# A 32-byte pool at the right end of SBUF, under the tiles that the MLP and the scan keep there

## The chip, the cores and the metric

One core of one Trainium2 chip runs the whole program in one launch. The metric is the device time of that launch in microseconds (us), the median of several runs; lower is better. The engines named below are TensorE (PE; its weight loads are listed apart as PEld), VectorE (DVE), ScalarE (ACT), GpSimd (POOL) and SyncE (SP), whose queue issues the transfers (DMA). SBUF is the on-chip memory of 128 partitions; an address below is a byte within a partition, the same for all partitions.

## The reference

One layer of a hybrid backbone for 128 context tokens and 2,048 latent tokens, model width 1,024. All numbers are float32.

```python
h = rmsnorm(x, norm_mix) * (1 + sc1) + sh1
o, s_new = mixer(h, ...)        # one input projection; 4 heads of a bidirectional gated
                                # DeltaNet beside 4 groups of a chunked gMLP; one output projection
x = x + ga1 * o
h = rmsnorm(x, norm_ffn) * (1 + sc2) + sh2
x = x + ga2 * (square(relu(h @ w_ff1)) @ w_ff2)     # w_ff1 1024 x 4096, w_ff2 4096 x 1024
y = rmsnorm(x, norm_final)
```

The six vectors sh1 to ga2 come from a conditioning vector through `silu(c) @ w_mod + b_mod`. The outputs are y for both sequences and the final scan states of the context.

## The kernel before, in words

**Matmuls.** A float32 operand is split into a high and a low part of a shorter float type (`fp32r`), and a product is three matmuls, high by high, high by low, low by high. The helper `mm3` issues them, so that its three lines, L217, L218 and L219, carry nearly all matmuls of the profile. Of a matmul's two operands the moving one is streamed through TensorE, column by column, and the other, 128 by 128, is loaded first as weights. In a profile row `f<-hop,zH` the tile `hop` moves and `zH` is the weight.

**Stages.** The tokens form 17 tiles of 128 (`NT`). The first stage, to about 440 us, normalizes and projects; its moving operands are kH and kL, 388 columns, from a pool with 24 slots. The scan stage, to about 1300 us, runs the DeltaNet chunks in both directions and fills gaps with the gMLP and the output projection; an order written out by hand (`WINDOWS`) sets which step comes when. Then comes the MLP in two halves.

**First half of the MLP** (`Unit`, from about 1300 to 2032 us): each of 32 units covers 256 columns of w_ff1 for one half of the latent tokens. A Strassen-like scheme makes seven products of a unit, in the order 1, 5, 6, 7, 3, 2, 4 (`ORDER`); each is four k-tiles of three matmuls of 512 columns, with the token side `hop` moving and the weight side split on the fly (`split4`, L1452: ScalarE L1456 makes the high part, VectorE L1450 the low part). The units run in 28 blocks of one or two. There are seven `hop` tiles for each half of the tokens, fetched by `hop_next`; products 1 and 5 use the right side, the others the left.

**Second half** (from 2032 us to the end): seven products in turn (numbers 1, 5, 6, 7, 3, 4, 2), each visited for 8 or 9 pairs of token tiles. A visit is four quarters of four k-tiles, twelve matmuls a quarter. Now w_ff2 moves, from `hop` tiles that `t_build` fills, four k-tiles in each (a chunk): ScalarE copies the high part (L1632), VectorE makes the low part. The token side (`zraw` to `zH`, `zL`) is loaded again for every quarter, `AHEAD` and two more quarters early. A product has four chunks, so chunks 0 to 27 in all.

**Pools.** SBUF tiles come from stacked pools. Those on the left grow up from the constants (`const`, `small`, `wp`, ...), those on the right grow down from the end. On the right lies the pool `prep` in the scan stage (half-precision tiles AH, As, X, Y, P and some float32 ones) and, once it is closed (`swap_right`), the pool `hopA` with two `hop` tiles of 16,384 bytes. `hopB`, with five, lies on the left:

```python
side, bufs = ("A", 2) if n else ("B", 5)
return hops[side].tile([P, 4, 2, 512], dt, tag="hop", name="hop", bufs=bufs)
...
moved.append(hop_tile(F32R, (len(tcount) - 1) % 5 < 2))
```

Slots are rounded up to multiples of 32 bytes. The usable part of a partition ends at byte 229,344, which is 3583 times 64 and 32 more. So before the change `hopA` takes bytes 196,576 to 229,344 and all 26 slots of `prep` start at 32 above a multiple of 64. The five `hopB` tiles (from byte 113,024), the slots of `wp` (from 12,672) and those of the scan's left pools start on multiples of 64.

The two constants that the change touches: `nhalf`, a row of -0.5 that GpSimd uses as the exponent in `rsqrt_cols` (L172), at most 72 columns of it; `zcol`, eight zeros, read in the first stage for `abW` (L302) and for edge columns of kH and kL (L453).

Of the kernel before, what the change touches and what calls it, by code (L numbers as in the profile page):

```python
# [8 lines left out]
F32 = mybir.dt.float32  # L9
# [8 lines left out]
P = 128  # L18
D = 1024
KT = D // P  # L20
# [41 lines left out]
def hybrid_step(  # L62
# [21 lines left out]
        return ap.bitcast(F32)  # L84

    cp = ctx.enter_context(tc.tile_pool(name="const", bufs=1))
    dp = ctx.enter_context(tc.tile_pool(name="dram", bufs=1, space=DRAM))


# [23 lines left out]
    make_identity(nc, ident)  # L113
    ident16 = cp.tile([P, P], F16, name="ident16")
    V.tensor_copy(ident16, ident)
    nhalf = cp.tile([P, 72], F32, name="nhalf")
    V.memset(nhalf, -0.5)
    zcol = cp.tile([P, KT], F32, name="zcol")
    V.memset(zcol, 0.0)
    bd2 = cp.tile([P, P], F16, name="bd2")  # L120
    om = {w: cp.tile([P, P], F16, name=f"om{w}") for w in (2, 4, 8, 16, 32)}
# [138 lines left out]
    with ExitStack() as ph:  # L260
# [478 lines left out]
        side = []  # L739
        for bi in range(len(BLOCKS)):  # L740
# [8 lines left out]
            for n, (gi, h) in enumerate(order):  # L749
# [40 lines left out]
                side = []  # L790
# [114 lines left out]
    with ExitStack() as ph:  # L905
        right = ctx.enter_context(ExitStack())
# [1031 lines left out]
```

## Time and profile before

| what | value |
|---|---|
| time, median of 3 runs | 2715.29 us (2714.51 to 2718.88) |
| the profiled execution, first to last instruction | 2715.6 us |
| TensorE busy | 2631.7 us, 97% |
| TensorE weight loads | 2195.9 us, 81% |
| VectorE busy | 1867.8 us, 69% |
| ScalarE busy | 1247.8 us, 46% |
| GpSimd busy | 226.4 us, 8% |
| moved by transfers | 580.91 MB, mean 214 GB/s |
| mean granted TensorE clock | 0.990 |

The page lists busy time by engine, then the span in slices, the transfer queues, the chain of work that ended last, and the costliest groups of instructions. A group's row gives line, engine, operation, out<-in, shape and count, then busy time and the mean of one in ns, then the idle time of the engine just ahead of them and what ended it. Matmuls are pipelined: one's duration covers its way through the array, and the next starts before it ends, so the pace is read from the distance between starts, in the timeline. Other answers of the trace used below are the waits (who waited for whom, us in total, times, longest) and the table of stretches (busy time of each engine in a stretch of the span).

### The profile page before, as it was taken

Reading aid. Unit: us, or ns where it says so; the run is one execution under the profiler, and the core shown is the slowest. Engines: PE = TensorE matmul, PEld = TensorE weight load, DVE = VectorE, ACT = ScalarE, POOL = GpSimd, SP = SyncE. Lnnn points to the kernel's source line nnn. Section 1 sums busy time; section 2 is a strip of 40 time slices with the busy share of each in tenths; the row PEclk is TensorE's granted clock in tenths of the full one; section 3 lists DMA queues with packets and bytes.
Section 4 is the critical chain, followed back from the end, with each engine's and each line's share of the span. In section 5 each row is a group of like instructions: output and inputs, shape, how many; then the busy total and the mean of one; then the engine's idle time right before and its main releaser. Section 6 shows DMA issues by size and latency. Waiting matters only on the chain.

```text
span 2715.6 us, 45142 instructions
## 1 busy us (share of the span) xinstructions
PE 2631.7 (97%) x15682; PEld 2195.9 (81%) x15682; DVE 1867.8 (69%) x3911; ACT 1247.8 (46%) x3092; POOL 226.4 (8%) x448
## 2 busy tenths in 40 slices
PE   8999999999999999899999999999999999999998
PEld 4999998787887777778888778888888787788887
DVE  5867655877777879885677857665565556775874
ACT  4655555555555567763355533332342432332441
POOL 3112113111111111110000000000000000000000
PEclk9999999999999989999999999999999999999999
DMA  8867539555555657885877796333459978776782
GB/s 293 281 198 223 184 119 293 170 159 152 165 160 167 196 174 244 276 271 179 286 222 231 212 311 206 111 110 106 122 166 364 336 257 300 272 240 215 231 262 90
DMA packets 569387, 580.91 MB, mean 214 GB/s; under 512 B 35692, under 2 KB 401692, under 8 KB 565574
## 3 DMA queue, kind: packets, MB, share of 16 engines
q1 hardware_dynamic: 569158, 578.03, 66.9%
q8 instruction: 123, 2.02, 0.3%
q14 instruction: 106, 0.87, 0.1%
HBM read 398.14 MB, written 179.74 MB: 213 GB/s over the span
## 4 chain that ended last, share of the span: by engine, by line
PE 82%; DMA 7%; DVE 6%; issue 2%; ACT 1%; SPq 1%; POOL 0%; DVEq 0%; POOLq 0%; ACTq 0%
PE f L219 16%; PE f L217 16%; PE f L218 16%; PE pj L217 6%; PE pj L219 6%; PE pj L218 6%; PE pd L952 2%; DMA qT<-qT_d 2%; PE pm L217 1%; PE pm L219 1%; PE pm L218 1%; PE pd L1131 1%; DMA raw<-in_w_mod_dram 1%; PE pd L1132 1%; PE pt L568 1%
## 5 line engine op out<-in xcount | busy, mean ns | idle before, releaser
L219 PE MATMUL f<-hop,zL 128*128 128x512 f32 x960 | 377.6, 394 | 1.7 <-DVE zL L1450 1.7
L217 PE MATMUL f<-hop,zH 128*128 128x512 f32 x960 | 377.4, 393 | 1.7 <-ACT zH L1456 1.7
L218 PE MATMUL f<-hop,zH 128*128 128x512 f32 x960 | 377.5, 394 | 0.0
L217 PE MATMUL f<-hop,wH 128*128 128x512 f32 x896 | 356.2, 398 | 6.1 <-ACT wH L1456 6.1
L218 PE MATMUL f<-hop,wH 128*128 128x512 f32 x896 | 352.2, 393 | 0.0
L219 PE MATMUL f<-hop,wL 128*128 128x512 f32 x896 | 352.1, 394 | 0.0
L1456 ACT CAST zH<-zraw 128x512 fp32r<-128x512 f32 x240 | 147.0, 620 | 291.3 <-DVE zraw L1450 90.8
L217 PEld LDWEIGHTS f<-hop,zH 128*128 128x128 f32 x960 | 180.6, 188 | 45.4 <-ACT zH L1456 3.4
L219 PEld LDWEIGHTS f<-hop,zL 128*128 128x128 f32 x960 | 180.7, 188 | 45.0 <-DVE zL L1450 3.5
L218 PEld LDWEIGHTS f<-hop,zH 128*128 128x128 f32 x960 | 180.7, 188 | 41.1
L1450 DVE TENSOR_TENSOR zL<-zraw,zH 128x512 fp32r<-128x512 f32 x240 | 162.6, 686 | 67.9 <-ACT zH L1456 52.6
L217 PEld LDWEIGHTS f<-hop,wH 128*128 128x128 f32 x896 | 169.6, 189 | 41.3 <-ACT wH L1456 6.5
L219 PEld LDWEIGHTS f<-hop,wL 128*128 128x128 f32 x896 | 169.2, 189 | 38.1 <-DVE wL L1450 0.3
L218 PEld LDWEIGHTS f<-hop,wH 128*128 128x128 f32 x896 | 169.4, 189 | 35.4
L217 PE MATMUL pj<-kH,wH 128*128 128x386 f32 (+2 forms) x568 | 190.6, 338 | 0.6 <-DVE kH L466 0.3
L219 PE MATMUL pj<-kH,wL 128*128 128x386 f32 (+2 forms) x568 | 190.3, 335 | 0.0
L218 PE MATMUL pj<-kL,wH 128*128 128x386 f32 (+2 forms) x568 | 189.5, 334 | 0.0
L176 POOL TENSOR_TENSOR r<-rsq,nhalf 128x1 f32<-128x1 f32 (+1 forms) x38 | 23.1, 607 | 1520.8 <-DVE rsq L175 1520.8
L516 DVE SCALAR_TENSOR_TENSOR cv<-pj,vec,cv 128x384 f32<-128x384 f32 (+2 forms) x164 | 87.1, 539 | 60.4 <-ACT cv L513 56.5
L1450 DVE TENSOR_TENSOR wL<-raw,wH 128x512 fp32r<-128x512 f32 x112 | 76.1, 687 | 76.3 <-ACT wH L1456 75.3
L217 PEld LDWEIGHTS pj<-kH,wH 128*128 128x128 f32 x568 | 107.2, 189 | 5.2 <-issue 4.7
L218 PEld LDWEIGHTS pj<-kL,wH 128*128 128x128 f32 x568 | 107.5, 189 | 0.5
(404 smaller groups left out, 6083.0 us busy)
## 6 DMA issues: line engine op xcount, KB each, us to landing
zraw<-z_d SPq DMA_DIRECT2D x212, 256.0 KB
raw<-in_w_ff_dram SPq DMA_DIRECT2D x128, 256.0 KB
hop<-hop_d SPq DMA_DIRECT2D x28, 1024.0 KB
z_d<-c SPq DMA_DIRECT2D x96, 256.0 KB
zraw<-s_d SPq DMA_DIRECT2D x96, 256.0 KB
raw<-in_w_mod_dram SPq DMA_DIRECT2D x80, 256.0 KB
r<-in_w_ff_dram SPq DMA_DIRECT2D x80, 256.0 KB
s_d<-s SPq DMA_DIRECT2D x64, 256.0 KB
```

The source lines that it names most:

```text
L176: G.tensor_tensor(out=out, in0=t[:np_, :n], in1=nhalf[:np_, :n], op=ALU.pow)
L217: T.matmul(ps, lh, rh, start=first and i == 0, stop=False, skip_group_check=more)
L218: T.matmul(ps, lh, rl, start=False, stop=False, skip_group_check=more)
L219: T.matmul(ps, ll, rh, start=False, stop=last and i == n - 1, skip_group_check=more)
L516: V.scalar_tensor_tensor(out=cv[:, o : o + m], in0=ps[:, s + sh : s + sh + m], scalar=convw[:, w, j : j + 1], in1=cv[:, o : o + m], op0=AL ...
L568: T.matmul(ps[:, i * P : (i + 1) * P], kTt[:, i * P : (i + 1) * P], rhs[:, i * P : (i + 1) * P], start=True, stop=True)
L952: T.matmul(p[:, h, :], lhs[:, h, :], rhs[:, h, :], start=True, stop=True)
L1131: T.matmul(p[:, h, :], u["qT"][:, h, :], s[:, h, :], start=True, stop=False)
L1132: T.matmul(p[:, h, :], u["QK"][:, h, :], u["vn"][:, h, :], start=s is None, stop=True)
L1450: V.tensor_tensor(out=out, in0=a, in1=b, op=op)
L1456: A.copy(h, src)
```

## The change

A pool `edge` is opened on the right side ahead of all others, and `zcol`, 32 bytes a partition, moves there from the left. `nhalf` grows from 72 to 80 columns, by the 32 bytes that `zcol` leaves, so that all later tiles on the left keep their addresses. All on the right lies 32 bytes lower: the 26 slots of `prep` and the two `hop` tiles of `hopA` (now bytes 196,544 to 229,312) start on multiples of 64.

```diff
     cp = ctx.enter_context(tc.tile_pool(name="const", bufs=1))
+    edge = ctx.enter_context(tc.tile_pool(name="edge", bufs=1, side="right"))
...
-    nhalf = cp.tile([P, 72], F32, name="nhalf")
+    nhalf = cp.tile([P, 80], F32, name="nhalf")
     V.memset(nhalf, -0.5)
-    zcol = cp.tile([P, KT], F32, name="zcol")
+    zcol = edge.tile([P, KT], F32, name="zcol")
     V.memset(zcol, 0.0)
```

## Prediction

> **What bounds the kernel now.** I read the page first, then the groups of instructions by shape, then the table of stretches, then TensorE's timeline in one stretch of the MLP, and last the waits. The page gives the span and, in 40 slices, how busy the transfer engines are:
>
> ```profile
> span 2715.6 us, 45142 instructions
> ...
> DMA  8867539555555657885877796333459978776782
> ```
>
> The span, 2715.6 us, is 0.3 us above the median of the three runs, 2715.29 us (2714.51 to 2718.88), so the sum below is made against the profile and taken off the median as it stands. Transfers are near their limit in only some slices, the 30th and 31st above all.
>
> The groups say what the MLP is made of, 2,880 matmuls of 512 columns in its second half and 2,688 in its first, with the big `hop` tile as the moving operand in each:
>
> ```profile
> L217 PE MATMUL f<-hop,zH 128*128 128x512 f32 x960 | 377.4, 393 | 1.7 <-ACT zH L1456 1.7
> L218 PE MATMUL f<-hop,zH 128*128 128x512 f32 x960 | 377.5, 394 | 0.0
> L217 PE MATMUL f<-hop,wH 128*128 128x512 f32 x896 | 356.2, 398 | 6.1 <-ACT wH L1456 6.1
> ```
>
> Idle time ahead of them is 1.7 and 6.1 us in all. The duration of a matmul (393 ns) is no pace: the next starts long before it ends. The stretches (first the length, then busy time of PE, PEld, DVE, ACT, POOL, each with a count; granted clock, share of the transfer engines, GB/s) tell where TensorE sets the pace and where it does not:
>
> ```profile
> 1500.00:1620.00 120.00, 115.67 (x508) 94.48 (x507) 82.88 (x138) 53.18 (x110) 1.93 (x3) 0.97 0.80 250
> 1700.00:1800.00 100.00, 100.00 (x536) 85.67 (x535) 59.81 (x94) 31.21 (x58) 0.00 (x0) 1.00 0.39 111
> 2050.00:2070.00 20.00, 20.00 (x88) 16.28 (x87) 10.36 (x15) 5.47 (x9) 0.00 (x0) 1.00 1.02 369
> 2110.00:2130.00 20.00, 18.93 (x81) 15.07 (x82) 11.74 (x20) 12.23 (x23) 0.00 (x0) 1.00 1.00 354
> 2310.00:2320.00 10.00, 10.00 (x46) 8.15 (x45) 10.00 (x17) 6.43 (x11) 0.00 (x0) 1.00 1.06 392
> 2320.00:2330.00 10.00, 7.73 (x23) 4.69 (x22) 10.00 (x17) 3.10 (x5) 0.00 (x0) 0.83 1.01 358
> ```
>
> At 1700 TensorE is busy throughout and transfers take 0.39: whatever shortens a matmul there shortens the kernel. At 2050 to 2130 the transfers are full, and at 2110 TensorE waits 1.07 us. At 2320 VectorE and the transfers are full and TensorE waits 2.27 us.
>
> **What the moving tile costs.** In the second half a `hop` tile holds a chunk of four k-tiles: `t_build` puts chunk c into the right pair when c mod 5 is below 2, into the left five otherwise. Product 5 (the second) owns chunks 4 to 7, so in each of its visits quarters 1 and 2 read from the right pair, quarters 0 and 3 from the left five. These rows (start, duration) lie in its second visit:
>
> ```profile
> 2150.23 0.39 PE L217 MATMUL f<-hop,zH 128*128 128x512 f32 x1
> ...
> 2153.03 0.40 PE L217 MATMUL f<-hop,zH 128*128 128x512 f32 x1
> ...
> 2155.79 0.39 PE L217 MATMUL f<-hop,zH 128*128 128x512 f32 x1
> ...
> 2158.51 0.40 PE L217 MATMUL f<-hop,zH 128*128 128x512 f32 x1
> ```
>
> Each row starts the next twelve matmuls. Quarter 2, right pair: 2.80 us, 233.3 ns each. Quarter 3, left, directly behind it: 2.76 us. Quarter 0 of the next visit, left: 2.72 us, 226.7 ns each. So the right pair costs 6.7 ns a matmul, and another 0.04 us each time that work comes back to the left. The operands have the same shape, weights and neighbours. What differs is the address. Worked out from the declared sizes, the right end of the usable partition is byte 229,344, which is 32 above a multiple of 64, so both right tiles (16,384 bytes each) begin 32 above one; the five left tiles begin on multiples of 64.
>
> **Offset or place?** The right pair also lies at the far end, so this pair of stretches alone does not say that the offset is guilty. The first stage has a case inside one pool: the 24 slots of tag `h` are 1,568 bytes, 24.5 times 64, so that they alternate between offsets 0 and 32, and kH and kL sit on opposite ones. A triple reads kH twice and kL once. In the block at 181 us kH has offset 32, in the block at 262 us offset 0:
>
> ```profile
> 181.31 0.34 PE L217 MATMUL pj<-kH,wH 128*128 128x386 f32 x1
> ...
> 187.71 0.27 PE L528 MATMUL pt<-ident,x 128*128 128x128 f32 x1
> ...
> 262.51 0.34 PE L217 MATMUL pj<-kH,wH 128*128 128x386 f32 x1
> ...
> 268.35 0.27 PE L528 MATMUL pt<-ident,x 128*128 128x128 f32 x1
> ```
>
> Twelve triples take 6.40 us, 533 ns each; eleven take 5.84 us, 531 ns each. One more displaced read in three costs 2 to 3 ns at 386 columns: the same sign, less than half the size. I take the offset as the cause, with this weak row as the reason to leave another possibility some chance.
>
> **The change, part by part.**
>
> *Constants.* zcol moves from the left to the new pool and nhalf grows by the 32 bytes that it leaves, so all that lies left of the stack stays where it is. One memset writes 80 columns for 72, once, at the start: nothing. The order in which tiles are asked for, the number of instructions and of transfers stay; no queue has a step moved past it and no wait is added.
>
> *The right pair goes from offset 32 to 0.* First half of the MLP: 32 units, of whose seven products two (1 and 5) read the right pair, twelve matmuls each: 768. Second half: chunks 0, 1, 5, 6, 10, 11, 15, 16, 20, 21, 25, 26, visited 9, 9, 8, 8, 8, 8, 9, 9, 8, 8, 9, 9 times: 102 visits of twelve, 1,224. Together 1,992 matmuls at 6.7 ns, 13.3 us. Returns to the left: one for each of 28 blocks of units, one for each of 60 visits; 88 at 0.04 us, 3.5 us. Gross 16.8 us, made of 3.1 (first half up to about 1620 us), 3.1 (1632 to 2032) and 10.6 (second half).
>
> *What hides part of it.* Where transfers are the limit, a faster TensorE only arrives early. Up to the wait behind 2110 us lie seven visits of product 1, each worth 24 times 6.7 ns and 0.04 us, 0.20 us: 1.4 us lost there, I take all of it, since the row at 2050 shows the transfers at 1.02. From 2310 us on VectorE and the transfers are full, up to the wait behind 2320; between nothing and the eight visits of the product before it, 1.6 us, I take 1.0. From 1303 to 1620 TensorE is busy 115.67 of 120 us in the row at 1500, with waits for other engines in between; of 3.1 us I take a third as lost, 1.0 (bounds 0 and 3.1). Late next at all three places is the same transfer or VectorE result as now, not a new one. Net 16.8 - 3.4 = 13.4 us, and 2715.3 - 13.4 = 2701.9, say 2702 us.
>
> *The tiles of the scan stage* on the right side (AH, As, X, Y, P and others, half-precision) move by the same 32 bytes. TensorE's reads of them have little room:
>
> ```profile
> 1217.93 0.28 PE L1038 MATMUL pd<-P,X 128*128 128x64 f16 x4
> 1218.04 0.28 PE L1040 MATMUL pd<-X,P 128*128 128x64 f16 x4
> 1218.16 0.28 PE L1038 MATMUL pd<-P,X 128*128 128x64 f16 x4
> 1218.28 0.28 PE L1040 MATMUL pd<-X,P 128*128 128x64 f16 x4
> ```
>
> Twelve in 0.35 us are 29.2 ns each; 64 columns at the left tiles' pace (226.7 ns for 512) would be 28.3. Of some 2,900 such matmuls that is at most 2.6 us, and TensorE waits for VectorE in that stage:
>
> ```profile
> PE pd L1038 <- DVE P L1029: 27.5, 32, 3.0
> ...
> PE f L836 <- DVE x L829: 6.4, 3, 4.3
> ```
>
> I take 0, and keep 0 to 2.6 us for the range. Element work does not care: ScalarE's four copies of a chunk into the left (first row, chunk 9) and into the right (second row, chunk 10) take the same 2.18 us, so nothing is gained or lost in building the tiles.
>
> ```profile
> 2214.18 2.18 ACT L1632 CAST hop<-traw 128x512 fp32r<-128x512 f32 x4 [2.13 <-PE f L219]
> ...
> 2216.99 2.18 ACT L1632 CAST hop<-traw 128x512 fp32r<-128x512 f32 x4
> ```
>
> The transfers into the right pair keep their sizes and count; the trace does not show the offset in them, and with a third of TensorE's gain already given up where they bind I cost them at nothing either way.
>
> **The rivals.**
>
> *Nothing moves.* The cost belongs to the far end of the memory, or to the pair's turn in the order, not to the offset. For it: the first-stage rows are only 2 to 3 ns apart. Against: those rows are in one pool, and the price starts with the first matmul on the right pair. Time 2715.3 us. A rule of the Trainium skill speaks for this case: "SBUF — State Buffer", in the section on the DMA port swizzle, has lines of 16 bytes, with a penalty only on crossing to a new line too often. An offset of 32 is as good a start as 0 by that rule, and the sum would be nothing, 2715.3 us. The rows at 2150 to 2158 do not agree as far as they go, 233.3 against 226.7 ns with contiguous reads in both, but they leave the place open.
>
> *The reads get faster, but the loads set the time.* Lost then are all of 1303 to 1620 (3.1 us), products 1 and 5 (17 visits, 3.4 us) and product 6 (1.6 us), 8.1 of 16.8. What is left is 8.7 us: 2706.6 us. For it: the transfers' 1.00 to 1.06 in the stretches shown. Against: TensorE waits there for only 1.07 and 2.27 us.
>
> *Slower: the scan chain pays for the new offset.* Its elementwise steps on the right tiles lie one behind the other, 170 of each of these:
>
> ```profile
> L1029 DVE SCALAR_TENSOR_TENSOR P<-pd,identq 128x256 f16<-128x256 f32 x170 | 70.4, 415 | 35.9 <-PE pd L1025 35.3
> ...
> L1042 ACT CAST X<-pd 128x256 f16<-128x256 f32 x170 | 65.7, 386 | 0.0
> ```
>
> To end 0.2% slower it must cost the 13.4 us of the gain and 5.4 us more, 18.8 us over 340 instructions: from 55 ns each on, 14% of 386. At that price the time is 2720.7 us. Against it: the equal copies at 2214 and 2216.
>
> **How the numbers follow.** About 0.2%, 5.4 us, is what a measurement of this kernel can tell from no change. The forecast, 2702 us, has 0.70; loads set the time 0.13; nothing moves 0.13; slower 0.04. Faster is then 0.83, the same 0.13, slower 0.04. The low end is the gross gain with nothing hidden and the scan's 2.6 us: 2715.3 - 19.4, 2695.9, taken as 2695.5. The high end takes in the case of the loads with some 2 us more: 2709.
>
> **What would show it.** Twelve matmuls on the right pair take 2.72 us as on the left, and the twelve behind them 2.72 instead of 2.76 us. The 896 and 960 groups lose a few ns of their mean. The wait near 2110 us grows by about 1.4 us, that near 2320 by about 1. ScalarE's and VectorE's durations on right tiles stay. Wrong it would be if the right pair kept 233 ns (place, not offset), if waits of more than 4 us appeared ahead of `zH`, `zL` or `wH`, or if L1029 and L1042 grew.

## The result, and the profile after

The changed kernel takes 2706.83 us (median of 11 runs, 2700.94 to 2713.28) against 2716.23 us (11 runs, 2711.70 to 2720.23): a ratio of 0.9967, 95% interval 0.9957 to 0.9977. That is 9.4 us by the medians, and 6.2 to 11.7 us by the interval; the two profiled executions are 6.6 us apart (2715.6 and 2709.0 us), a figure that the noise of single executions, several us, also moves. No engine has another order of instructions. Added lines move line numbers by one or two: L217 to L219 of before are L218 to L220 after.

From the page after:

```profile
span 2709.0 us, 45142 instructions
...
L218 PE MATMUL f<-hop,zH 128*128 128x512 f32 x960 | 378.5, 395 | 2.4 <-ACT zH L1457 2.4
L220 PE MATMUL f<-hop,zL 128*128 128x512 f32 x960 | 377.2, 393 | 1.7 <-DVE zL L1451 1.7
L219 PE MATMUL f<-hop,zH 128*128 128x512 f32 x960 | 374.7, 391 | 0.0
L218 PE MATMUL f<-hop,wH 128*128 128x512 f32 x896 | 356.6, 398 | 6.9 <-ACT wH L1457 6.9
```

One group's mean fell by 3 ns, its sister rose by 2: a duration says little of the pace. The timeline says more; this is the same place of the program as in the prediction (start, duration; each row starts the next twelve matmuls):

```profile
2145.60 0.40 PE L218 MATMUL f<-hop,zH 128*128 128x512 f32 x1
...
2148.35 0.40 PE L218 MATMUL f<-hop,zH 128*128 128x512 f32 x1
...
2151.12 0.39 PE L218 MATMUL f<-hop,zH 128*128 128x512 f32 x1
...
2153.84 0.40 PE L218 MATMUL f<-hop,zH 128*128 128x512 f32 x1
```

The twelve on the right pair take 2.75 us, 229 ns each (2.80 before, 2.72 on the left). The twelve behind them take 2.77 us (2.76 before): the price of coming back has stayed. TensorE's waits of over 0.2 us in the second half follow, before the change and then after it. In square brackets stands how long the engine sat idle, and who ended that:

```profile
2111.07 0.50 PE L217 MATMUL f<-hop,zH 128*128 128x512 f32 x1 [1.19 <-ACT zH L1456]
2322.23 0.50 PE L217 MATMUL f<-hop,zH 128*128 128x512 f32 x1 [0.52 <-ACT zH L1456]
2324.71 0.67 PE L219 MATMUL f<-hop,zL 128*128 128x512 f32 x1 [1.75 <-DVE zL L1450]
```

```profile
2096.84 0.50 PE L218 MATMUL f<-hop,zH 128*128 128x512 f32 x1 [0.27 <-ACT zH L1457]
2106.80 0.50 PE L218 MATMUL f<-hop,zH 128*128 128x512 f32 x1 [1.19 <-ACT zH L1457]
2316.63 0.50 PE L218 MATMUL f<-hop,zH 128*128 128x512 f32 x1 [0.93 <-ACT zH L1457]
2319.11 0.80 PE L220 MATMUL f<-hop,zL 128*128 128x512 f32 x1 [1.74 <-DVE zL L1451]
```

The wait near 2110 is 1.19 us in both (the prediction's 1.07 is the part of it that lies behind 2110.00); a wait of 0.27 us is new ahead of it. Near 2320 the two waits grew from 2.27 to 2.67 us, and ahead of `wH`, in the groups, 6.1 became 6.9. ScalarE's copies into the left (first row) and right (second row) tiles are as they were:

```profile
2209.04 2.18 ACT L1633 CAST hop<-traw 128x512 fp32r<-128x512 f32 x4 [2.13 <-PE f L220]
...
2211.80 2.19 ACT L1633 CAST hop<-traw 128x512 fp32r<-128x512 f32 x4
```

So the change did what it says to the addresses, and the right pair became faster, by about 4.4 ns a matmul instead of 6.7. Why not all of it?

### The profile page after: what moved, and what is told of

Read it like the earlier page. It is cut to its first block, busy times and chain, and to the rows that moved or that the text cites. A ratio compares the mean times of both kernels' runs of the same rounds, so it can differ in the third digit from the quotient of the medians.

```text
span 2709.0 us, 45142 instructions
## 1 busy us (share of the span) xinstructions
PE 2624.9 (97%) x15682; PEld 2197.2 (81%) x15682; DVE 1867.7 (69%) x3911; ACT 1246.2 (46%) x3092; POOL 225.7 (8%) x448
## 4 chain that ended last, share of the span: by engine, by line
PE 76%; DMA 12%; DVE 7%; ACT 2%; issue 2%; SPq 1%; POOL 0%; DVEq 0%; POOLq 0%; ACTq 0%
PE f L218 15%; PE f L220 15%; PE f L219 15%; PE pj L218 6%; PE pj L220 5%; PE pj L219 5%; DMA qT<-qT_d 2%; PE pd L953 2%; DMA raw<-in_w_mod_dram 1%; PE pm L218 1%; PE pm L220 1%; PE pm L219 1%; DMA hop_d<-opH 1%; DMA r<-in_w_ff_dram 1%; PE pt L569 1%
## 5 line engine op out<-in xcount | busy, mean ns | idle before, releaser
L218 PE MATMUL f<-hop,zH 128*128 128x512 f32 x960 | 378.5, 395 | 2.4 <-ACT zH L1457 2.4
L220 PE MATMUL f<-hop,zL 128*128 128x512 f32 x960 | 377.2, 393 | 1.7 <-DVE zL L1451 1.7
L219 PE MATMUL f<-hop,zH 128*128 128x512 f32 x960 | 374.7, 391 | 0.0
L218 PE MATMUL f<-hop,wH 128*128 128x512 f32 x896 | 356.6, 398 | 6.9 <-ACT wH L1457 6.9
L219 PE MATMUL f<-hop,wH 128*128 128x512 f32 x896 | 351.7, 393 | 0.0
L220 PE MATMUL f<-hop,wL 128*128 128x512 f32 x896 | 351.7, 393 | 0.0
L220 PEld LDWEIGHTS f<-hop,zL 128*128 128x128 f32 x960 | 180.8, 188 | 45.6 <-DVE zL L1451 3.0
L218 PEld LDWEIGHTS f<-hop,zH 128*128 128x128 f32 x960 | 180.9, 188 | 43.6 <-ACT zH L1457 3.7
L219 PEld LDWEIGHTS f<-hop,zH 128*128 128x128 f32 x960 | 180.8, 188 | 39.4
L218 PEld LDWEIGHTS f<-hop,wH 128*128 128x128 f32 x896 | 169.8, 189 | 41.0 <-ACT wH L1457 7.3
L220 PEld LDWEIGHTS f<-hop,wL 128*128 128x128 f32 x896 | 169.3, 189 | 37.6 <-DVE wL L1451 0.3
L219 PEld LDWEIGHTS f<-hop,wH 128*128 128x128 f32 x896 | 169.8, 190 | 34.1
L218 PE MATMUL pj<-kH,wH 128*128 128x386 f32 (+2 forms) x568 | 191.0, 339 | 0.3 <-DVE kH L467 0.3
L220 PE MATMUL pj<-kH,wL 128*128 128x386 f32 (+2 forms) x568 | 190.9, 336 | 0.0
L219 PE MATMUL pj<-kL,wH 128*128 128x386 f32 (+2 forms) x568 | 190.0, 335 | 0.0
L218 PEld LDWEIGHTS pj<-kH,wH 128*128 128x128 f32 x568 | 107.5, 190 | 4.6 <-issue 4.2
L219 PEld LDWEIGHTS pj<-kL,wH 128*128 128x128 f32 x568 | 108.0, 190 | 0.5
```

Of the source, the lines that this page charges most:

```text
L218: T.matmul(ps, lh, rh, start=first and i == 0, stop=False, skip_group_check=more)
L219: T.matmul(ps, lh, rl, start=False, stop=False, skip_group_check=more)
L220: T.matmul(ps, ll, rh, start=False, stop=last and i == n - 1, skip_group_check=more)
```

## The experiments

Theory A: the boundary that counts is coarser than 64 bytes. Theory B: the rest is the price of the place. Later a third joined them, theory R: what counts is no boundary at all, but the distance between the moving tile and the weights. (The expectations below call A the absolute or offset theory, B the place theory and R the relative theory.) The right tiles began at byte 196,576 before and 196,544 after the change; divided by 512 they leave 480 and 448. All slots of the weights' pool, and the five left tiles, leave 384. A remainder of 384 on division by 512 is called "384 by 512" below.

**Four sizes and places.** All are edits of the changed kernel:

```diff
-    zcol = edge.tile([P, KT], F32, name="zcol")
+    zcol = edge.tile([P, 24], F32, name="zcol")[:, :KT]    # 96 bytes; 56: 224 bytes; 16: 64 bytes
```

96 bytes:

> The pool at the right end takes 96 bytes instead of 32, so both right hop tiles start on a multiple of 128 (byte 196,480), as the left five do (113,024 is 883 times 128). Theory A (a coarser boundary, 128 bytes, sets the 2 to 3 ns that the changed kernel still pays on the right pair): 12 matmuls on the right pair take 2.72 us instead of the changed kernel's 2.74 to 2.75; some 1,992 x 2.5 ns = 5 us less than the changed kernel, 0.5% less than before in all (ratio near 0.995). Theory B (the rest is the price of the place at the far end): pace and time as the changed kernel, 0.9967.

Measured: 2700.12 us, ratio 0.9941 (0.9926 to 0.9956), lower than the changed kernel's whole interval. The timeline, with the right pair's second twelve first:

```profile
2131.04 0.39 PE L218 MATMUL f<-hop,zH 128*128 128x512 f32 x1
...
2133.76 0.39 PE L218 MATMUL f<-hop,zH 128*128 128x512 f32 x1
...
2136.48 0.39 PE L218 MATMUL f<-hop,zH 128*128 128x512 f32 x1
```

Twelve on the right pair and the twelve on the left behind them both take 2.72 us: both prices are gone. Place is ruled out, as the pair lies where it did but for 64 bytes.

224 bytes:

> The pool takes 224 bytes: the right hop tiles start on a multiple of 256 (byte 196,352), the left five at 128 above one. Theory A with 128 as the boundary: as with 96 bytes, 2.72 us for 12 matmuls, ratio near 0.995. If what counts is an equal remainder to the left tiles and the weights (128 above a multiple of 256), the rest of 2 to 3 ns stays and the ratio is near 0.9967. Theory B (place): also 0.9967.

Measured: 2709.74 us, 0.9974 (0.9964 to 0.9983), and 2.80 us for the right pair's second twelve, the pace of before the change, though these tiles start on a multiple of 256:

```profile
2134.78 0.40 PE L218 MATMUL f<-hop,zH 128*128 128x512 f32 x1
...
2137.58 0.39 PE L218 MATMUL f<-hop,zH 128*128 128x512 f32 x1
...
2140.31 0.39 PE L218 MATMUL f<-hop,zH 128*128 128x512 f32 x1
```

By the pace, theory A falls; the remainder by 512 is 256 here, 384 with 96 bytes. The time does not say so: it is 5.7 us below that of before and its interval overlaps the changed kernel's. The twelve behind, on the left, take 2.73 us where they took 2.76, so that coming back costs 0.01 instead of 0.04 us; for 88 returns that is some 2.6 us by estimate. What the rest comes from, no run here shows.

64 bytes:

> The pool takes 64 bytes: the right tiles are 32 above a multiple of 64 again (byte 196,512), with the pool still there. Offset theory: 12 matmuls on the right pair take 2.80 us as before the change, ratio 1.000. If the pool itself or zcol's new place brought the gain, the pace is the changed kernel's and the ratio 0.9967.

Measured: 2714.05 us, 0.9994 (0.9983 to 1.0005), twelve in 2.80 us. The pool by itself brings nothing.

The left five moved instead:

```diff
+    gap = ctx.enter_context(tc.tile_pool(name="gap", bufs=1, reuse_waits="tile"))
+    G.memset(gap.tile([P, 8], F32, name="gap"), 0.0)
     hops["B"] = ctx.enter_context(tc.tile_pool(name="hopB", bufs=1, reuse_waits="tile"))
```

> The changed kernel, and a 32-byte tile below the left five hop tiles, which now start 32 above a multiple of 64 (byte 113,056); weights and right pair as in the changed kernel. Offset theory: the 5,568 - 1,992 = 3,576 matmuls on left tiles rise from 226.7 to 233 ns, +24 us, less what waits hide: ratio 1.004 to 1.006 against before. Place theory: the left stays at 226.7 ns and the ratio at 0.9967.

Measured: 2721.67 us, 1.0025 (1.0013 to 1.0037). The left twelve rose to 2.80 us, so the left too is slow once it is displaced. Against the changed kernel's 0.9967 the ratio rose by 0.0058, about 16 us of the 24, less than expected. Where the rest went is not shown.

**Boundary or distance.** The weights had stood still so far. To move them, nhalf grows by 8 columns more, which pushes all on the left 32 bytes up; with a right pool of 64 bytes everything keeps its distance and nothing is on a multiple of 64:

```diff
-    nhalf = cp.tile([P, 80], F32, name="nhalf")
+    nhalf = cp.tile([P, 88], F32, name="nhalf")
...
-    zcol = edge.tile([P, KT], F32, name="zcol")
+    zcol = edge.tile([P, 16], F32, name="zcol")[:, :KT]
```

> nhalf takes 32 bytes more on the left and the right pool 64 bytes, so that weights, left five and right pair all start 32 above a multiple of 64, with one remainder by 512 (416) for moving tiles and weights alike. Absolute theory (an address off the multiples of 64 is slow, wherever the weights are): all 5,568 matmuls of the MLP at about 233 ns, ratio 1.008 to 1.012. Relative theory (a moving tile is slow when its remainder by 512 differs from that of the weights): all at 226.7 ns though none lies on a multiple of 64, ratio as with the 96-byte pool, 0.994.

Measured: 2701.58 us, 0.9955 (0.9942 to 0.9967), and in its timeline the right pair runs as fast as the left:

```profile
2131.20 0.39 PE L218 MATMUL f<-hop,zH 128*128 128x512 f32 x1
...
2133.92 0.39 PE L218 MATMUL f<-hop,zH 128*128 128x512 f32 x1
```

Twelve in 2.72 us. Absolute alignment falls. The same left side with the right pair back on a multiple of 128 (pool of 96 bytes):

> Weights and left five as in the run above (416 by 512), right pair on a multiple of 128 (384 by 512). Absolute theory: right pair at 226.7 ns, left five at 233 ns, ratio 1.002 to 1.006. Relative theory: just the other way round, left five 226.7 ns, right pair 233 ns, ratio 1.000 (as before the change).

Measured: 2713.20 us, 0.9997 (0.9988 to 1.0006). The first two rows begin the right pair's two quarters, the third a left quarter of the next visit, the fourth what follows it:

```profile
2132.25 0.40 PE L218 MATMUL f<-hop,zH 128*128 128x512 f32 x1
...
2135.05 0.40 PE L218 MATMUL f<-hop,zH 128*128 128x512 f32 x1
...
2140.60 0.39 PE L218 MATMUL f<-hop,zH 128*128 128x512 f32 x1
...
2143.32 0.40 PE L218 MATMUL f<-hop,zH 128*128 128x512 f32 x1
```

The aligned right pair takes 2.80 us (first two rows), the left quarter at 2140, which is not aligned, 2.72: just the other way round from theory A. Two more distances, with right pools of 352 and 160 bytes:

> As the changed kernel with 352 bytes in the pool: right pair at 128 by 512, weights at 384, a difference of 256. If the relation repeats every 256 bytes: 226.7 ns on the right pair, ratio 0.994. If it takes 512: about 233 ns, ratio 0.998 to 1.000. Absolute theory (128 above a multiple of 256 is good): 226.7 ns.

Measured: 2701.01 us, 0.9955 (0.9939 to 0.9970), twelve in 2.72 us: a distance of 256 is as good as none.

> 160 bytes in the pool: right pair at 320 by 512, 64 below the weights' 384, where the changed kernel has 64 above. If the sign of the difference does not matter: 229 ns on the right pair, as in the changed kernel. If it does: 231 to 233 ns.

Measured: one run, 2718.76 us, and twelve in 2.80 us: 64 below is not as good as 64 above.

**The disputed cost by itself.** The series stand in one loop of 36 (`count`), with the displacements `d` of the moving tile and `w` of the weights, in bytes, in the tiles' offsets:

```python
size = 2 if half else 4
a, b = (m16, w16) if half else (mv, wt)
ps = psq.tile([P, 512], F32, tag="f", name=name, bufs=8)
for i in range(count):
    o = w // size + (i % 4) * 512 // size
    T.matmul(ps[:, :n], b[:, o : o + P], a[:, d // size : d // size + n], start=i == 0, stop=i == count - 1)
```

> Leaves out the whole computation: series of 36 matmuls (128 x 512, each with its own weight load, nothing else running), a series for each displacement of the moving tile (m, bytes) and of the weights (w, bytes) from one common remainder by 512; f is the split float32 type, h half-precision, n fewer columns. Relative theory with a period of 256 bytes: 226.7 ns a matmul where m - w is 0 or 256 (also m32w32, m64w64, m32w288), 229 at +64, 233 at +-32, 96, 128. Absolute theory: m32w32 as slow as m32w0, m0w32 as fast as m0w0. If the cost comes from VectorE's, ScalarE's or the transfers' traffic and not from the weights, all series have one pace.

Its timeline merges a series into one row (start, duration to the end of the last one, count). The pace is the distance to the next row's start, by 36:

```profile
42.42 8.32 PE L95 MATMUL m0w0f<-mv,wt 128*128 128x512 f32 x36
50.58 8.68 PE L95 MATMUL m4w0f<-mv,wt 128*128 128x512 f32 x36
59.10 8.55 PE L95 MATMUL m8w0f<-mv,wt 128*128 128x512 f32 x36
...
75.83 8.56 PE L95 MATMUL m32w0f<-mv,wt 128*128 128x512 f32 x36
84.23 8.55 PE L95 MATMUL m48w0f<-mv,wt 128*128 128x512 f32 x36
92.62 8.40 PE L95 MATMUL m64w0f<-mv,wt 128*128 128x512 f32 x36
100.86 8.49 PE L95 MATMUL m80w0f<-mv,wt 128*128 128x512 f32 x36
109.19 8.57 PE L95 MATMUL m96w0f<-mv,wt 128*128 128x512 f32 x36
117.60 8.56 PE L95 MATMUL m128w0f<-mv,wt 128*128 128x512 f32 x36
...
209.40 8.56 PE L95 MATMUL m0w64f<-mv,wt 128*128 128x512 f32 x36
217.80 8.53 PE L95 MATMUL m0w128f<-mv,wt 128*128 128x512 f32 x36
...
250.77 8.36 PE L95 MATMUL m32w32f<-mv,wt 128*128 128x512 f32 x36
258.96 8.35 PE L95 MATMUL m64w64f<-mv,wt 128*128 128x512 f32 x36
267.14 8.36 PE L95 MATMUL m128w128f<-mv,wt 128*128 128x512 f32 x36
...
307.80 7.93 PE L95 MATMUL m32w0h<-mv,wt 128*128 128x512 f16 x36
315.57 7.93 PE L95 MATMUL m64w0h<-mv,wt 128*128 128x512 f16 x36
323.34 7.93 PE L95 MATMUL m128w0h<-mv,wt 128*128 128x512 f16 x36
```

Without displacement 8.16 us, 226.7 ns each. Moving tile by 32: 8.39 to 8.40 us, 233 ns. By 64: 8.24 us, 228.9 ns, the changed kernel's pace. By 96: 8.41 us, 233.6 ns, the pace of before. By 4: 8.52 us, 236.7 ns. The weights by 64, so that the moving tile is 64 below: 8.40 us, 233.3 ns. Both by 32 or both by 64: 8.18 to 8.19 us, and no series with equal remainders by 256 is slower than 8.21 us, 228.1 ns. With nothing else running the prices are the kernel's own, so VectorE, ScalarE and the transfers are not needed for them. Half-precision does not care: 7.77 us, 215.8 ns, with the moving tile displaced by 32, 64 or 128, 7.79 us without. The series with fewer columns show no price either: displaced by 32, 64 or 128, 128 columns take 4.02 to 4.03 us and 256 columns 4.24 to 4.27; undisplaced, 4.15 and 4.36, the first series of each width, which also bears the switch to it.

**Aligned and slow.** In the kernel, with the right pool of 96 bytes and the left side 32 bytes up, a gap of 480 bytes brings the left five to 384 by 512; only what lies below them, the weights with it, is displaced:

> The kernel itself, all seven hop tiles on multiples of 128 (384 by 512), and only the weights' pool, with all else of the left stack below the hop tiles, 32 bytes higher (416 by 512). Absolute theory: as the 96-byte pool, ratio 0.994. Relative theory: all 5,568 matmuls of the MLP at 233 ns, though their moving tiles are aligned: about 24 us over the time before, ratio 1.004 to 1.009.

Measured: 2726.41 us, 1.0057 (1.0039 to 1.0075), the slowest kernel of all, with every moving tile of the MLP on a multiple of 128. From the right pair's second twelve to the left ones behind it:

```profile
2138.38 0.40 PE L218 MATMUL f<-hop,zH 128*128 128x512 f32 x1
...
2141.18 0.40 PE L218 MATMUL f<-hop,zH 128*128 128x512 f32 x1
...
2143.98 0.40 PE L218 MATMUL f<-hop,zH 128*128 128x512 f32 x1
```

2.80 us on the right, 2.80 us on the left.

**The same cure in the first stage**, beside the pool of 96 bytes:

```diff
-                kH = p1.tile([P, 388], F32R, tag="h", name="kH", bufs=24)
+                kH = p1.tile([P, 448], F32R, tag="h", name="kH", bufs=24)[:, :388]      # kL alike
```

> The 96-byte pool, and in the first stage kH and kL padded from 388 to 448 columns, so that their 24 slots (now 1,792 = 7 x 256 bytes apart, before 1,568) all have the weights' remainder by 256; before, slot k lay 32 k bytes off it, by 256. Relative theory: the 1,704 matmuls of the first stage drop from a mean near 177.5 to 174 ns, up to 6 us more, ratio 0.992. If the relation does not matter at 386 columns: as the 96-byte pool alone, 0.994.

Measured: 2698.37 us, 0.9948 (0.9935 to 0.9960), which the 96-byte pool's 0.9941 (0.9926 to 0.9956) does not differ from. So the 6 us more did not come. The two blocks that the prediction timed, in the padded kernel:

```profile
181.15 0.34 PE L218 MATMUL pj<-kH,wH 128*128 128x386 f32 x1
...
187.50 0.27 PE L529 MATMUL pt<-ident,x 128*128 128x128 f32 x1
...
261.93 0.34 PE L218 MATMUL pj<-kH,wH 128*128 128x386 f32 x1
...
267.76 0.38 PE L529 MATMUL pt<-ident,x 128*128 128x128 f32 x2
```

Twelve triples take 6.35 us and eleven 5.83, 529 and 530 ns a triple; with the 96-byte pool alone they take 6.40 and 5.84 us, as before the change. At 386 columns the distance is worth about 1 ns a matmul in these blocks, too little for the kernel's time to show.

## Why the prediction was right, and where not

The direction, the place and the range held: 2706.83 us lies in 2695.5 to 2709. The size and the reason did not: 9.4 us by the medians for a forecast of 13.4, and the offset from a multiple of 64 is not what slows a tile. Point by point:

- **The price of the right pair** (6.7 ns a matmul, 0.04 us a return) was read rightly. The step that failed is "The right pair goes from offset 32 to 0": it took for granted that a multiple of 64, which the left tiles have, is what makes them fast. The left tiles are fast since they have the weights' remainder. The change moved the right pair from 96 to 64 above that, from 233.3 to 229 ns. 1,992 times 4.4 ns is 8.8 us, in place of 13.3, and the 3.5 us of the returns stayed where they were. That a step of 32 bytes helped at all was luck: of the other multiples of 64, 64 below the weights' remainder (the 160-byte pool) and 128 below it (224 bytes) leave the twelve at 2.80 us.
- **The reason given for the step** was an argument from two places that differ in many things. The 96-byte, 224-byte and all-displaced kernels part them: 384 by 512 is fast, 256 by 512 is slow, and 416 is fast when the weights have it too.
- **What hides part of it** was put at 3.4 us of 16.8. How much of the 8.8 was hidden, the runs do not tell: the measured gain, 6.2 to 11.7 us, allows nothing and more than 2 us. The two profiles cannot settle it. The first matmul of the MLP starts at 1303.49 us before and at 1300.60 after, so that 2.9 of their 6.6 us lie ahead of it, and the 64-byte kernel, which is no faster than before, also left a profile of only 2709.5 us. Place by place: near 2110, where all of 1.4 us was to be lost, the wait stayed at 1.19 us and one of 0.27 appeared ahead of it; near 2320 it grew by 0.4 for 1.0; ahead of `wH` by 0.8 for 1.0.
- **The sum with its own premise made true.** Where the remainders by 256 match, the kernels with pools of 96 and 352 bytes are 0.59% and 0.45% faster than before, 12 to 16 us; the 13.4 us forecast lies between.
- **The first-stage rows** were offered as a weak case of the offset. They were none: slots 1,568 bytes apart lie 32 bytes on by 256 each, so that both blocks mixed many distances. With one remainder for all slots the blocks take 529 and 530 ns a triple, so the 2 to 3 ns between them may come from the mix; a single execution of each does not settle that.
- **Nothing from the scan stage, nothing from element work:** held. The half-precision series do not care, the copies take 2.18 and 2.19 us, and the 170 instructions of each of the two scan groups take 416 and 386 ns on the mean after the change, 415 and 386 before.
- **The signs.** Twelve on the right pair were to take 2.72 us and took 2.75; those behind them were to take 2.72 and took 2.77. The 896 and 960 groups were to lose a few ns of their mean, and only one of the rows shown did, so that this sign was no use.
- **Rivals.** "Nothing moves" fell; of its two grounds, place is ruled out by the 96-byte kernel. The Trainium skill's lines of 16 bytes ("SBUF — State Buffer", section on the DMA port swizzle) do not tell these cases apart: 32, 64 and 96 are multiples of 16 and cost 233, 229 and 233.6 ns. "The loads set the time", 2706.6 us, gave nearly the measured number for a wrong reason: with the right distance the same loads let 12 to 16 us through. The number alone would have backed a wrong account.

## What to carry to other kernels

When one of two pools of like tiles is slower, compare the distance between starts of a dozen matmuls, not their mean duration, and list both operands' addresses before naming a cause: here it was the distance of the moving tile from the weights, modulo 256 bytes, and not the alignment of either. Of such float32-split matmuls with 512 columns, give the moving tiles and the weights the same remainder by 256; a pad in the pool stack does it. At 386 columns it was worth about 1 ns a matmul, and at 128 and 256 columns and in half-precision no price was seen. And test the reason by moving the other operand: the aligned kernel with displaced weights was the slowest of all.

## What the runs showed of the hardware

A matmul of 512 columns with split float32 operands goes at 226.7 to 228.1 ns when moving tile and weights have one remainder by 256 bytes, at 228.9 to 229.2 ns when the moving tile is 64 above, and at 231 to 237 ns at the other distances tried; the sign counts (64 below: 233 ns). In half-precision it goes at 216 ns, displaced or not. Why the two addresses matter to each other, and why 64 above is cheaper than 64 below, no run here shows.
